# Attention scores in 4 MB tiles: turning keys and queries with 32x32 word blocks on VectorE instead of TensorE transposes

## The chip, the cores and the metric

The kernel runs on one core of a Trainium2 chip. The metric is the device time of one execution in microseconds (us), the median over several runs of the same program. One further execution is taken with the hardware profiler; its own time and span stand in the table below.

## What is computed

```
batch, heads, seq, dim = 8, 8, 512, 64
scale = 1.0 / np.sqrt(q.shape[-1])
return (np.einsum('bhqd,bhkd->bhqk', q, k) * scale).astype(np.float32)
```

For each of the 64 heads (8 batches of 8) a 512 x 512 matrix of scaled dot products is made from 512 queries and 512 keys of 64 elements. The inputs q and k are 8.39 MB each, the output is 67.11 MB, all float32 in DRAM.

## The kernel before

**Units, loads, words.** Two batches make a unit, and there are four (`UNITS`). A unit's keys and queries come in with one transfer of 2 MB each (`load`, L82; the very first is split in two halves, L87, one on SyncE's queue and one on ScalarE's). Each of the 128 partitions gets 64 consecutive rows of one head, 16 KB in one piece; partition p holds piece p of the unit in DRAM order (`k_r`, `q_r`). GpSimd casts them to bfloat16 (L131, 16 casts of 2048 elements a partition) and lays two rows side by side, so that one 32-bit word holds the same element of two rows (`xb`). A transpose that moves 32-bit words thus turns two rows at once. Each load's casts raise `ready` by one when they are done.

**Turning.** TensorE contracts over partitions, so keys and queries must lie with their 64 elements along partitions. `turn` (L139) transposes eight 128 x 128 blocks of words on TensorE, with an identity matrix that GpSimd makes at the start (L108 and L110), into a PSUM tile (`tp`; at the start also the score tiles). A unit has four such chunks, two of keys and two of queries. `move` (L191) copies each chunk from PSUM into `kT` (keys) and `qz` (queries): ScalarE copies one half and VectorE the other, two copies each. `qz` is zero outside its blocks (two memsets, L197), so that one matmul over 128 partitions makes 64 queries of two heads, whose keys lie in the upper and lower 64 partitions of `kT`.

**Scores and output.** The output is written in 16 tiles of 4 MB, four heads each (`out_r`). A tile has eight pairs of matmuls (`scores`, L154); each pair fills one of three PSUM tiles (`ps`, 128 x 1024 float32). ScalarE takes the even pairs (L218) and VectorE the odd ones (L221): they scale and write to one of three SBUF buffers of 4 MB (`big`). SyncE (SP) waits for both engines' four drains (L100 and L101) and stores the tile with one transfer (L102). The three `big` buffers also receive the loads of the units (`xf`), the second of them twice.

**What sets the order.** Everything is written out by hand, engine by engine, with semaphores. SP's queue holds the loads, then the wait for casts that free the buffer of the last unit's two loads, then the 16 stores in order. A tile's buffer is free when its casts are done (tiles 0 to 2) or the store three tiles earlier has landed; TensorE waits for that itself, between the two matmuls of the tile's first pair. In tile g, TensorE also turns chunk g + 4 after the third pair (while there is one), and both drain engines move it between their drains.

Of the kernel before, what the change touches and what calls it, by code (L numbers as in the profile page):

```python
# [5 lines left out]
def kernel(  # L6
# [5 lines left out]
    nc = tc.nc  # L12
    B, H, S, D = q.shape
    scale = 1.0 / (D ** 0.5)
    P = 128
    UNITS = B // 2
    N = H
    M = P // (2 * H)
    R = S // M
    J = R // 2  # L20
    RO = 8
    U = S // RO
    JP = J // 2
    JJ = J // RO // 2
    W = 8
    IW = W // JJ
    TILES = N // 2
    CHUNKS = 4
    SLOTS = 12
    PAIRS = RO  # L30

    f32 = mybir.dt.float32
    bf16 = mybir.dt.bfloat16
    mult = mybir.AluOpType.mult


    names = ["ready", "moved", "zeroed", "ident", "turn", "pe_act", "pe_dve", "act", "dve"]
    sem = {name: nc.alloc_semaphore(name) for name in names}
    load_sems = [nc.alloc_semaphore(f"load{n}") for n in range(2 * UNITS)]
    halves = [load_sems[0], nc.alloc_semaphore("load0b")]  # L40
    store_sems = [nc.alloc_semaphore(f"store{n}") for n in range(3)]
    ALL = CHUNKS * UNITS

    q_r = q.rearrange("(v b) g (m j) d -> v (b g m) (j d)", b=2, j=R)
    k_r = k.rearrange("(v b) g (m j) d -> v (b g m) (j d)", b=2, j=R)
    out_r = out.rearrange("(v b) (t x h) (u i) k -> (v b t) (h u) x (i k)", b=2, x=2, h=2, i=RO)

    bigs = [nc.alloc_sbuf_tensor(f"big{n}", [P, 2, RO, S], f32)[:] for n in range(3)]
    xb = nc.alloc_sbuf_tensor("xb", [P, SLOTS * W, 2, D, 2], bf16)[:]
    kT = nc.alloc_sbuf_tensor("kT", [P, 2 * N, M, 2, J], bf16)[:]  # L50
    qz = nc.alloc_sbuf_tensor("qz", [P, 2 * N, RO, P], bf16)[:]
    identity = nc.alloc_sbuf_tensor("identity", [P, P], f32)[:]
    tp = nc.alloc_psum_tensor("tp", [P, W, P], f32)[:]
    pss = [nc.alloc_psum_tensor(f"ps{n}", [P, 2, S], f32)[:] for n in range(3)]

    def words(ap):
        return ap.bitcast(f32)

    def half(h):
        return slice(h * D, (h + 1) * D)  # L60

    kw = words(kT)
    qw = words(qz)
    xw = words(xb.rearrange("p w s d e -> p w (s d e)"))
    keys = kT.rearrange("p n m s j -> p n (m s j)")

    pe = nc.tensor

# [4 lines left out]
    def store_buffer(g):  # L75
        return bigs[(0, 2, 1)[g % 3]]

    def rows(v, x):
        return (k_r, q_r)[x][v].rearrange("p (s c) -> p s c", s=2)

    def load(v, x):
        nc.sync.dma_start(out=xf(v)[:, x], in_=rows(v, x)).then_inc(load_sems[2 * v + x], 16)  # L82

    for s, queue in enumerate((nc.sync, nc.scalar)):
        first_load = queue.dma_start(out=xf(0)[:, 0, s], in_=rows(0, 0)[:, s]  # L87
                                     ).then_inc(halves[s], 16)
        tc.no_tile_sem_insts.add(first_load.ins.name)
    tc.close()  # L90
    tc.compile()  # L91


    for n in range(1, 2 * (UNITS - 1)):
        load(n // 2, n % 2)
    for x in range(2):
        nc.sync.wait_ge(sem["ready"], 3 + x)
        load(UNITS - 1, x)
    for g in range(ALL):
        nc.sync.wait_ge(sem["act"], 4 * g + 4)  # L100
        nc.sync.wait_ge(sem["dve"], 4 * g + 4)  # L101
        nc.sync.dma_start(out=out_r[g], in_=store_buffer(g).rearrange("p x i k -> p x (i k)")  # L102
                          ).then_inc(store_sems[g % 3], 16)
    for n in range(3):
        nc.sync.wait_ge(store_sems[n], 16 * len(range(n, ALL, 3)))


    nc.gpsimd.memset(identity, 0.0).then_inc(sem["ident"], 1)  # L108
    nc.gpsimd.wait_ge(sem["ident"], 1)
    nc.gpsimd.affine_select(out=identity, in_=identity, compare_op=mybir.AluOpType.not_equal,  # L110
                            fill=1.0, base=0, pattern=[[-1, P]], channel_multiplier=1
                            ).then_inc(sem["ident"], 1)
    for v in range(UNITS):
        for x in range(2):
            w0 = (v * CHUNKS + 2 * x) % SLOTS * W
            if v or x:
                nc.gpsimd.wait_ge(load_sems[2 * v + x], 16)
            if v == UNITS - 1 and x == 0:
                nc.gpsimd.wait_ge(sem["turn"], CHUNKS)
            for s in range(2):  # L120
                if v == x == 0:
                    nc.gpsimd.wait_ge(halves[s], 16)
                src = xf(v)[:, x, s]
                dst = xb[:, w0:w0 + JP, s]
                if x == 0:
                    src = src.rearrange("p (j e d) -> p j e d", e=2, d=D)
                    dst = dst.rearrange("p j d e -> p j e d")
                else:
                    src = src.rearrange("p (j e i d) -> p j e i d", e=2, i=RO, d=D)
                    dst = dst.rearrange("p (i j) d e -> p j e i d", i=RO)  # L130
                cast = nc.gpsimd.tensor_copy(out=dst, in_=src)  # L131
            cast.then_inc(sem["ready"], 1)


    first = [tp] + [ps.rearrange("p w (c k) -> p (w c) k", k=P) for ps in pss]

    def turn(c, dst):
        for w in range(W):
            ins = pe.transpose(out=dst[:, w], identity=identity, in_=xw[:, c % SLOTS * W + w])  # L139
        ins.then_inc(sem["turn"], 1)  # L140

    def scores(g, p):
        x, i = p // 4, p % 4 * 2
        n = g % (2 * TILES) * 2 + x
        pair = PAIRS * g + p
        if pair >= 3:
            pe.wait_ge(sem["act" if p % 2 else "dve"], (pair - 3) // 2 + 1)
        for w in range(2):
            if p == 0 and w == 1:
                if g < 3:  # L150
                    pe.wait_ge(sem["ready"], (2, 6, 8)[g])
                else:
                    pe.wait_ge(store_sems[g % 3], g // 3 * 16)
            ins = pe.matmul(out=pss[pair % 3][:, w, :], lhsT=qz[:, n, i + w], rhs=keys[:, n],  # L154
                            start=True, stop=True)
        ins.then_inc(sem["pe_dve" if p % 2 else "pe_act"], 1)

    pe.wait_ge(sem["ident"], 2)
    for c in range(CHUNKS):
        if c % 2 == 0:  # L160
            pe.wait_ge(sem["ready"], c // 2 + 1)
        turn(c, first[c])
    pe.wait_ge(sem["moved"], 2)
    for g in range(ALL):
        c = g + CHUNKS
        for p in range(3):
            scores(g, p)
        if c < ALL:
            pe.wait_ge(sem["ready"], c // 2 + 1)
            turn(c, tp)  # L170
        for p in range(3, PAIRS):
            scores(g, p)

    def move(copy, c, s, tile_):
        v, t = divmod(c, CHUNKS)
        n0 = v % 2 * N
        h0 = t % 2 * W
        if t < 2:  # L180
            src = tile_[half(s)].rearrange("d j (n h m) -> d h n m j", n=N, h=2)
        else:
            src = tile_[half(s)].rearrange("d (i jj) (n h m) -> d h i n m jj", jj=JJ, n=N, h=2)
            h0 = t % 2 * IW
        for h in range(2):
            if t < 2:
                dst = kw[half(h), n0:n0 + N, :, s, h0:h0 + W]
            else:
                dst = qw[half(h), n0:n0 + N, h0:h0 + IW, h * U // 2:(h + 1) * U // 2].rearrange(
                    "d n i (m s jj) -> d s i n m jj", s=2, jj=JJ)[:, s]  # L190
            last = copy(out=dst, in_=src[:, h])  # L191
        return last

    def evacuator(engine, copy, scaled, parity, done, freed):
        if parity:
            for v in range(2):
                engine.memset(qz[:, v * N:(v + 1) * N], 0.0).then_inc(sem["zeroed"], 1)  # L197
        for c in range(CHUNKS):
            engine.wait_ge(sem["turn"], c + 1)
            if c == 2:  # L200
                engine.wait_ge(sem["zeroed"], 2)
            last = move(copy, c, parity, first[c])
        last.then_inc(sem["moved"], 1)
        count = 0
        for g in range(ALL):
            o = store_buffer(g)
            for p in range(parity, PAIRS, 2):
                x, i = p // 4, p % 4 * 2
                count += 1
                engine.wait_ge(done, count)  # L210
                scaled(o[:, x, i:i + 2, :], pss[(PAIRS * g + p) % 3]).then_inc(freed, 1)
                c = g + CHUNKS
                if p in (1, 2) and c < ALL:
                    engine.wait_ge(sem["turn"], c + 1)
                    move(copy, c, parity, tp)

    evacuator(nc.scalar, nc.scalar.copy,
              lambda o, ps: nc.scalar.mul(out=o, in_=ps, mul=scale),  # L218
              0, sem["pe_act"], sem["act"])
    evacuator(nc.vector, nc.vector.tensor_copy,  # L220
              lambda o, ps: nc.vector.tensor_scalar(out=o, in0=ps, scalar1=scale, scalar2=None,  # L221
                                                    op0=mult),
              1, sem["pe_dve"], sem["dve"])


# [28 lines left out]
```

## Time and profile before

| quantity | value |
|---|---|
| median of 3 runs | 201.21 us (201.21 to 202.08) |
| profiled execution, whole time | 201.47 us |
| profiled execution, span | 200.1 us |
| busy TensorE, VectorE, ScalarE, GpSimd | 100.0, 106.1, 84.8, 39.5 us |
| matmuls for scores (L154) | 256 issued, 249 recorded, 456 ns each |
| mean granted TensorE clock | 0.81 of full speed |
| transfers | 83.95 MB, mean 420 GB/s over the span |
| SP's store issues (L102) | 16, of 4096 KB, 0.37 us each |

The span is what the profiler covers; the whole time holds some 1.4 us more. A line number such as L154 is the line of the kernel that issued the instruction. Busy time of an engine that nobody waits for costs nothing; the view called the chain of waits follows back, from the last instruction, what each step was released by.

### The profile page before, as it was taken

What the parts mean: (1) busy time and instruction counts of PE and PEld (TensorE: products, weight loads), DVE (VectorE), ACT (ScalarE), POOL (GpSimd) and SP (SyncE); (2) the same over time, 40 slices, a digit from 0 to 9 for tenths busy, and PEclk for the clock granted to TensorE, in tenths of its full rate; (3) what the DMA queues carried; (4) which work ended last, traced back from release to release, by engine and by line L of the source; (5) the groups of instructions that cost most, each with busy time, mean ns of one, the idle gap of its engine ahead of it and who ended that gap; (6) DMA issues with size and microseconds to landing.
All of it is one profiled execution on the core that took longest, in us unless ns stands there. A gap on an engine that the chain in (4) does not pass through costs nothing.

```text
span 200.1 us, 1063 instructions
## 1 busy us (share of the span) xinstructions
PE 100.0 (50%) x377; PEld 47.2 (24%) x384; DVE 106.1 (53%) x98; ACT 84.8 (42%) x97; POOL 39.5 (20%) x22
## 2 busy tenths in 40 slices
PE   0027760376674757654764486366747374830000
PEld 0026530143231414311431243042202120200000
DVE  4815592076993757691769276829454435450000
ACT  2004671265773746572666266546444344430000
POOL 1299999995000000000000000000000000000000
PEclk9999997579998888995799679969697858585555
DMA  6999999999999999999999999999999999999995
GB/s 188 434 432 439 432 426 426 426 406 442 426 422 426 449 431 421 426 442 432 422 422 439 436 429 422 439 436 429 422 426 449 429 422 422 439 436 426 429 429 252
DMA packets 5653, 83.95 MB, mean 420 GB/s; under 512 B 400, under 2 KB 400, under 8 KB 400
## 3 DMA queue, kind: packets, MB, share of 16 engines
q1 hardware_dynamic: 5504, 82.84, 97.4%
q10 hardware_dynamic: 144, 1.05, 1.3%
q8 instruction: 3, 0.05, 0.1%
q14 instruction: 2, 0.02, 0.0%
HBM read 16.78 MB, written 67.11 MB: 419 GB/s over the span
## 4 chain that ended last, share of the span: by engine, by line
DMA 56%; DVE 12%; PE 10%; POOL 10%; issue 1%; SPq 0%
DMA out_dram<-big 43%; POOL xb L131 10%; DVE big L221 9%; PE ps L154 8%; DMA big<-in_k_dram 7%; DMA big<-in_q_dram 6%; PE tp L139 2%; DVE qz L191 2%; DVE kT L191 1%; SPq L101 0%
## 5 line engine op out<-in xcount | busy, mean ns | idle before, releaser
L154 PE MATMUL ps<-kT,qz 128*128 128x512 bf16 x249 | 80.2, 456 | 61.8 <-DMA out_dram<-big 32.4
L221 DVE TENSOR_SCALAR big<-ps 128x1024 f32<-128x1024 f32 x64 | 76.9, 1222 | 52.9 <-PE ps L154 48.6
L218 ACT ACTIVATE big<-ps 128x1024 f32<-128x1024 f32 x64 | 65.0, 1023 | 71.8 <-PE ps L154 66.4
L154 PEld LDWEIGHTS ps<-kT,qz 128*128 128x128 bf16 x256 | 25.3, 110 | 109.8 <-DMA out_dram<-big 35.8
L131 POOL CAST xb<-big 128x2048 bf16<-128x2048 f32 x16 | 38.8, 2467 | 6.5 <-DMA big<-in_k_dram 6.2
L139 PE MATMUL tp<-identity,xb 128*128 128x128 f32 x104 | 18.8, 341 | 13.7 <-POOL xb L131 13.7
L139 PEld LDWEIGHTS tp<-identity,xb 128*128 128x128 f32 x104 | 17.2, 185 | 17.7 <-issue 16.6
L191 DVE COPY kT<-tp 64x512 f32<-64x512 f32 x14 | 9.7, 694 | 10.2 <-PE tp L139 9.9
L191 ACT COPY kT<-tp 64x512 f32<-64x512 f32 x14 | 8.1, 577 | 14.8 <-PE tp L139 14.7
L191 DVE COPY qz<-tp 64x512 f32<-64x512 f32 x12 | 8.3, 694 | 3.0 <-PE tp L139 2.7
L197 DVE MEMSET qz<- 128x4096 uint32 x2 | 6.9, 3472 | 3.6 <-PEq L91 2.8
L191 ACT COPY qz<-tp 64x512 f32<-64x512 f32 x12 | 7.5, 624 | 1.2 <-PE tp L139 1.1
L139 PE MATMUL ps<-identity,xb 128*128 128x128 f32 x24 | 5.6, 421 | 1.2 <-POOL xb L131 1.2
L139 PEld LDWEIGHTS ps<-identity,xb 128*128 128x128 f32 x24 | 5.0, 226 | 1.6 <-POOL xb L131 1.6
L191 DVE COPY qz<-ps 64x512 f32<-64x512 f32 x4 | 2.8, 695 | 2.1 <-PE ps L139 2.1
L191 ACT COPY qz<-ps 64x512 f32<-64x512 f32 x4 | 2.5, 625 | 2.5 <-PE ps L139 2.4
L191 ACT ACT_TABLE_LOAD x1 | 1.3, 1283 | 1.9 <-PEq L91 1.9
L191 DVE COPY kT<-ps 64x512 f32<-64x512 f32 x2 | 1.4, 694 | 0.3 <-PE ps L139 0.3
L191 ACT COPY kT<-ps 64x512 f32<-64x512 f32 x2 | 1.2, 578 | 0.6 <-PE ps L139 0.5
L108 POOL MEMSET identity<- 128x128 f32 x1 | 0.2, 204 | 1.5 <-POOLq L91 1.5
L110 POOL TENSOR_SCALAR_AFFINE_SELECT identity<-identity 128x128 f32<-128x128 f32 x1 | 0.3, 293 | 0.2 <-POOL identity L108 0.2
L238 POOL MEMSET const-float32-0.0<- 128x1 f32 x1 | 0.1, 98 | 0.2 <-issue 0.2
(3 smaller groups left out, 0.3 us busy)
## 6 DMA issues: line engine op xcount, KB each, us to landing
out_dram<-big SPq DMA_DIRECT2D x16, 4096.0 KB, 21.5
big<-in_q_dram SPq DMA_DIRECT2D x4, 2048.0 KB, 17.6
big<-in_k_dram SPq DMA_DIRECT2D x3, 2048.0 KB, 16.2
big<-in_k_dram ACTq DMA_DIRECT2D x1, 1024.0 KB, 8.2
big<-in_k_dram SPq DMA_DIRECT2D x1, 1024.0 KB, 8.0
```

What stands on the lines that cost most here:

```text
L108: nc.gpsimd.memset(identity, 0.0).then_inc(sem["ident"], 1)
L110: nc.gpsimd.affine_select(out=identity, in_=identity, compare_op=mybir.AluOpType.not_equal, fill=1.0, base=0, pattern=[[-1, P]], channel_m ...
L131: cast = nc.gpsimd.tensor_copy(out=dst, in_=src)
L139: ins = pe.transpose(out=dst[:, w], identity=identity, in_=xw[:, c % SLOTS * W + w])
L154: ins = pe.matmul(out=pss[pair % 3][:, w, :], lhsT=qz[:, n, i + w], rhs=keys[:, n], start=True, stop=True)
L191: last = copy(out=dst, in_=src[:, h])
L197: engine.memset(qz[:, v * N:(v + 1) * N], 0.0).then_inc(sem["zeroed"], 1)
L218: lambda o, ps: nc.scalar.mul(out=o, in_=ps, mul=scale),
L221: lambda o, ps: nc.vector.tensor_scalar(out=o, in0=ps, scalar1=scale, scalar2=None, op0=mult),
L238: nc = _bacc.Bacc("TRN2", target_bir_lowering=False, num_devices=1)
```

## The change

Loads and stores stay at the same sizes and counts, and so do casts, matmuls and drains. The order of rows in the loads, the path that turns keys and queries, and the control of the score loop are new:

- **Loads.** A partition still gets 64 consecutive rows (16 KB). But partition 64s + 32h + 4m + 2b + x now holds piece m of head 4x + 2s + h of batch b of the unit, so each quadrant of 32 partitions holds 8 pieces of 4 heads. The four partitions of a group (2b + x) read DRAM rows that are 512 KB apart, and the next group starts 16 KB further on. Output tiles hold heads two of which lie 4 heads apart (2 before).
- **Turning.** `turn`, `move`, the identity and `tp` are gone. VectorE transposes 32 x 32 blocks of words straight from `xb` to `kT` and `qz` in SBUF: per two tiles, two instructions for keys (64 partitions x 1024 words) and four for queries (32 partitions x 1024 words). The output is written with a step of 1 KB between neighbouring words for keys, 2 KB for queries. `kT` and `qz` are half as large; one memset remains. The transposes for the next two tiles are spread over VectorE's queue by `after`: in an even tile one after drain 1, one after drain 4, two after drain 6; in an odd tile two after drain 1.
- **Drains.** There are four PSUM score tiles. ScalarE takes five pairs of each tile, VectorE three (`takers`).
- **Loop.** TensorE runs a loop of four rounds over four tiles, with counters that are lowered again in the loop. SP, after issuing a tile's store, waits until the next tile's buffer is free and then raises `next0` or `next1`, for which TensorE waits at the tile's first matmul.

```diff
-    q_r = q.rearrange("(v b) g (m j) d -> v (b g m) (j d)", b=2, j=R)
-    k_r = k.rearrange("(v b) g (m j) d -> v (b g m) (j d)", b=2, j=R)
-    out_r = out.rearrange("(v b) (t x h) (u i) k -> (v b t) (h u) x (i k)", b=2, x=2, h=2, i=RO)
+    q_r = q.rearrange("(v b) (x s h) (m j) d -> v (s h m) (b x) (j d)", b=2, x=2, s=2, j=R)
+    k_r = k.rearrange("(v b) (x s h) (m j) d -> v (s h m) (b x) (j d)", b=2, x=2, s=2, j=R)
+    out_r = out.rearrange("(v b) (x s h) (u i) k -> v s b (h u) x (i k)", b=2, x=2, s=2, i=RO)
...
+    takers = ["act", "dve", "act", "act", "dve", "act", "dve", "act"]
...
+        nc.sync.wait_ge(sem["out"], 2 * (g + 1))
+        nc.sync.dma_start(out=out_r[g // 4, g // 2 % 2, g % 2],
+                          in_=store_buffer(g).rearrange("p x i k -> p x (i k)")
                           ).then_inc(store_sems[g % 3], 16)
+        if g < ALL - 1:
+            if g < 2:
+                nc.sync.wait_ge(sem["ready"], (6, 8)[g])
+            else:
+                nc.sync.wait_ge(store_sems[(g + 1) % 3], (g + 1) // 3 * 16)
+            nc.sync.sem_inc(sem[f"next{(g + 1) // 2 % 2}"], 1)
...
-    def turn(c, dst):
-        for w in range(W):
-            ins = pe.transpose(out=dst[:, w], identity=identity, in_=xw[:, c % SLOTS * W + w])
-        ins.then_inc(sem["turn"], 1)
...
+    with pe.Fori(0, ALL // 4):
+        for t in range(4):
+            two, r = divmod(t, 2)
+            for p in range(PAIRS):
+                n, i = t * 2 + p // 4, p % 4 * 2
+                if p == 0:
+                    pe.wait_ge(sem[f"next{two}"], r + 1)
+                elif p >= 4:
+                    name, count = frees[p - 4]
+                    pe.wait_ge(sem[f"{name}{two}"], r * (3 if name == "act" else 1) + count)
+                for w in range(2):
+                    ins = pe.matmul(out=pss[p % 4][:, w, :], lhsT=qz[:, n, i + w], rhs=kT[:, n],
+                                    start=True, stop=True)
...
+    def turn_keys(b, y):
+        s = b % 2 * 2 * Q
+        return nc.vector.transpose(
+            out=kw[2 * y * Q:2 * (y + 1) * Q, b % 2 * G:(b % 2 + 1) * G].rearrange(
+                "d g (m w) -> d w m g", w=J),
+            in_=xw[s:s + 2 * Q, b // 2 * 2, :, y * Q:(y + 1) * Q])
+
+    def turn_queries(b, y, h):
+        s = (b % 2 * 2 + h) * Q
+        d = (2 * y + h) * Q
+        return nc.vector.transpose(
+            out=qw[d:d + Q, b % 2 * G:(b % 2 + 1) * G, :, h * Q:(h + 1) * Q].rearrange(
+                "d g i (m jj) -> d i jj m g", jj=JJ),
+            in_=xw[s:s + Q, b // 2 * 2 + 1, :, y * Q:(y + 1) * Q].rearrange(
+                "p (i jj) d -> p i jj d", i=RO))
...
+    after = {(0, 1): 1, (0, 4): 1, (0, 6): 2, (1, 1): 2}
...
-        for h in range(2):
-            if t < 2:
-                dst = kw[half(h), n0:n0 + N, :, s, h0:h0 + W]
-            else:
-                dst = qw[half(h), n0:n0 + N, h0:h0 + IW, h * U // 2:(h + 1) * U // 2].rearrange(
-                    "d n i (m s jj) -> d s i n m jj", s=2, jj=JJ)[:, s]
-            last = copy(out=dst, in_=src[:, h])
-        return last
```

## The prediction

> **What bounds the kernel now.** I read the profile in this order: the slices of the span, the transfers, the chain of waits, then the groups of instructions. The slices come first because one row of them has no gap.
>
> ```profile
> PE   0027760376674757654764486366747374830000
> DVE  4815592076993757691769276829454435450000
> DMA  6999999999999999999999999999999999999995
> HBM read 16.78 MB, written 67.11 MB: 419 GB/s over the span
> ```
>
> Each digit is a 5 us slice in tenths. TensorE and VectorE come and go; the transfer engines are full from the second slice to the last but one. So I asked whether they run at one rate. The windows view (columns: window and length; busy time and count of PE, PEld, DVE, ACT, POOL; clock; DMA share; GB/s) says yes, in loads and in stores:
>
> ```profile
> 5.00:15.00 10.00, 1.25 (x6) 1.28 (x7) 4.79 (x2) 0.00 (x0) 6.12 (x3) 1.00 1.02 434
> 38.00:42.00 4.00, 3.86 (x14) 2.50 (x15) 1.23 (x1) 2.05 (x2) 3.92 (x3) 0.50 1.00 401
> 100.00:150.00 50.00, 29.92 (x114) 13.20 (x114) 31.52 (x30) 25.84 (x29) 0.00 (x0) 0.86 1.00 430
> ```
>
> 83.95 MB at 430 GB/s are 195.2 us; with some 2.8 us before the first byte (the first slice moves 188 x 5 = 940 KB, 2.2 us at 430) and 2.1 us after the last that is the span, 200.1 us. The chain of waits shows how far compute is from the limit:
>
> ```profile
> 61.78 21.31 DMA out_dram<-big
> 83.09 0.04 issue
> 83.14 1.25 PE ps L154 x5
> ...
> 86.72 3.59 DVE big L221 x3
> 90.31 0.02 issue
> 90.32 0.02 SPq L101
> 90.34 0.03 issue
> 90.37 21.91 DMA out_dram<-big
> ```
>
> A tile waits for its buffer's store to land (83.1), is computed in 7.2 us and issues its own store at 90.3, which lands after 21.9 us. A 4.19 MB store needs 9.75 us at 430 GB/s. What an issue costs beside the bytes follows from the first load: 2.1 MB issued at 0.74, first cast at 8.79, so 8.05 - 2.1/0.434 = 3.2 us. The other 21.9 - 9.75 - 3.2 = 9 us it stood in the queue: that is slack. Over all stores:
>
> ```profile
> DMA to landing us min/median/max: 16.5/21.5/23.0
> ```
>
> So the thinnest slack is 16.5 - 9.75 - 3.2 = 3.5 us. Compute costs nothing until it is that late, and a lasting loss needs more than 9.75 us a tile.
>
> **The change, part by part.** These rows give the prices (count, then busy us and mean ns of one):
>
> ```profile
> L221 DVE TENSOR_SCALAR big<-ps 128x1024 f32<-128x1024 f32 x64 | 76.9, 1222 | 52.9 <-PE ps L154 48.6
> L218 ACT ACTIVATE big<-ps 128x1024 f32<-128x1024 f32 x64 | 65.0, 1023 | 71.8 <-PE ps L154 66.4
> L131 POOL CAST xb<-big 128x2048 bf16<-128x2048 f32 x16 | 38.8, 2467 | 6.5 <-DMA big<-in_k_dram 6.2
> L139 PE MATMUL tp<-identity,xb 128*128 128x128 f32 x104 | 18.8, 341 | 13.7 <-POOL xb L131 13.7
> L191 DVE COPY kT<-tp 64x512 f32<-64x512 f32 x14 | 9.7, 694 | 10.2 <-PE tp L139 9.9
> L197 DVE MEMSET qz<- 128x4096 uint32 x2 | 6.9, 3472 | 3.6 <-PEq L91 2.8
> ```
>
> *Removed:* 128 TensorE transposes (18.8 + 5.6 us), 32 copies on each of VectorE (22 us) and ScalarE (19 us), one memset (3.5 us), the identity. All of it ends in the 9 us of slack, except at the start, costed below.
>
> *Added on VectorE:* 48 transposes of 1024 words a partition. No such row exists. Low end: the memset's rate, 3472/4 = 0.87 us. High end: a word is two bf16, and GpSimd's cast writes 2048 bf16 in 2.47 us. I take 1.22 us, the L221 row, which is nearest: same engine, 1024 words. The output pattern steps 1 KB between words; L191 read PSUM with a 512-byte step: from it to L221 are 528 ns for 512 words more, 1.03 ns a word, which leaves 694 - 528 = 0.17 us fixed in both, so that step cost nothing per word. VectorE's drains fall from 4 to 3 a tile: 3 x 1.22 + 3 x 1.22 = 7.3 us a tile, against 4 x 1.22 + 2 x 0.69 = 6.3 now. ScalarE has five drains, 5.1 us. TensorE's 16 matmuls stand 0.43 us apart at the half clock (loads of weights at 38.54, 38.97, 39.39 and 39.82 in the timeline; the window from 38 to 42 shows 0.50), 6.9 us, and one drain, so 8.1. All are under 9.75.
>
> *Start.* Query casts end at 18.6; VectorE has four query transposes left, 4.9 us, to 23.5 (first score now: 23.8). Tile 0: 1.2 us to its first bank, then three drains and two key transposes, 6.1 us, so its store goes out near 31 (now 31.25). Loads fill the queue to 2.8 + 16.78/0.430 = 42. Tiles 1 and 2 start when GpSimd's casts free their buffers (38.1, 48.0), as now, and take about 7.5 us: issued at 46 and 55.5, with the queue full to 51.7 and 61.5. Nothing runs dry. What is late next if it did: the buffer's own landing, so each later tile.
>
> *Moved:* SP, not TensorE, now waits for a buffer's store and then raises a semaphore; TensorE's first matmul of a tile, ScalarE and VectorE's first drain stand behind that. SP does it after its own store issue (0.37 us), so queued behind the wait is only the next store, which cannot be ready earlier. Say 0.2 us a tile; the 9 us cover it, without them it is 15 x 0.2 = 3 us. The wait for the last two loads keeps its place. The transposes wait for casts, with VectorE's drains queued behind them; these waits are met before they are reached (the casts end at 47.9, tile 2 starts at 48.0). GpSimd's wait for the first turns goes; no row of the waits shows that it held anything. The loop's branch falls between tiles, under the same cover.
>
> *Loads.* Same bytes, same 16 KB rows, but neighbouring partitions now read rows 512 KB apart, in a pattern with one more dimension. Issue: loads now take 0.33 to 0.53 us; the first stands at 0.39, so 0 to 0.14 us, all on the path; I take 0.1. Rate: no load of this kind is in the trace; the windows bound it by 434 (0.4 us less over 16.78 MB) and 401 GB/s (2.8 us more). I take no change, since the stores, in two pieces 2 MB apart, run at 430 as well as the loads.
>
> The Trainium skill speaks against this, in "DMA: Bandwidth & Descriptors", section "Latency and other measured facts": with rows 512 KiB apart from partition to partition it gives 207 GB/s in each direction where a padded layout has 214. This trace has no such load. By it the loads would take 3% longer, an estimate of 1.3 us from that page, and the sum would be 202.7.
>
> **Sum.** 200.1 + 0.1 - 0 = 200.2 span; with the 1.37 us around the profiled span (201.47 - 200.1) 201.57. The runs' median lies 0.26 under the profiled run, so 201.3; I say 201.4, for tiles that start a little late. Its own range is 200.3 to 202.2.
>
> **The rivals.**
> *Slower, loads.* The transfer engines read the new row order less well. For it: they have no spare time, so each 1% of load rate costs 0.39 us; 0.5% (1 us) is reached below 420 GB/s. Against: descriptors stay 16 KB. At 401 GB/s: 204.2. If rows crowd on half of the engines, 39 us more: 240.
> *Slower, transposes.* A pair of tiles has 6 drains and 6 transposes and 1.2 us until VectorE's first bank; two stores take 19.5 us, so it decides from (19.5 - 7.3 - 1.2)/6 = 1.83 us a transpose. At 2.47 us: 23.3 - 19.5 = 3.8 us, over seven pairs 27, less about 6 of slack: 222. For it: a step of 1 KB at each word written, which no VectorE row has. Against: L191's strided reads.
> *Faster, transfers.* If new addresses ran everything at the best window's 434: 83.95/434 is 1.8 us less, 199.6. Against: the stores' rows are as before but for pieces 4 MB apart instead of 2.
> *Not what it says.* If the copies had been on the end's path, removing them would gain; the chain passes them in the 7.2 us only, which wait in the queue anyway: 201.4.
>
> **How the numbers follow.** Forecast 0.48 (0.05 of it the last rival, which gives the same time); loads slower 0.25; transposes slower 0.14; transfers faster 0.13. A change under 0.5% (200.2 to 202.2) can't be told from none. So faster 0.13, same 0.48, slower 0.39. For the range I leave out transposes well above 1.83 us and crowded loads (0.16) and 0.04 below: 199.6 to 212. Likeliest: 201.4.
>
> **What will show it.** The DMA row stays 9s throughout; the first store goes out near 31 us; landing times keep a minimum above 13 us; transposes near 1.2 us; load windows at 430. Wrong if a digit under 9 stands inside the row (compute late), or if it is full at a lower GB/s in the first 42 us (loads).

## The result, and the profile after

The changed kernel takes 208.71 us (median of 4 runs, 208.47 to 209.88) against 201.34 us for the kernel before in the same comparison: 3.7% slower, ratio 1.037 with a 95% interval of 1.0323 to 1.0416. The profiled execution spans 207.5 us. That lies inside the range of the prediction, but not in its likeliest case: the rival "slower, transposes" came.

First, the slices of the span and the sums of the page, as they were read before:

```profile
DVE  3338969995999599959996899779996999265000
DMA  5999999999999999999997999799979998899998
HBM read 16.78 MB, written 67.11 MB: 404 GB/s over the span
DVE 68%; PE 9%; DMA 5%; POOL 3%; ACT 3%; SPq 2%; issue 1%; DVEq 0%
```

The transfer row, full to the end before, now falls to 7 or 8 from the 22nd slice on, about once for every pair of tiles, and VectorE's row is nearly full. A digit under 9 inside the transfer row is what the prediction named as the sign that compute comes late. The last line, the shares of the chain that ended last by engine, turned round: DMA had 56% and VectorE 12%, now VectorE has 68% and DMA 5%. The groups of instructions say why (count, then busy us and mean ns of one):

```profile
L199 DVE TENSOR_SCALAR big<-ps 128x1024 f32<-128x1024 f32 x48 | 57.8, 1219 | 22.5 <-PE ps L146 22.2
L165 DVE STREAM_TRANSPOSE qz<-xb 32x1024 f32<-32x1024 f32 x32 | 64.2, 2005 | 1.2 <-POOL xb L126 0.8
L157 DVE STREAM_TRANSPOSE kT<-xb 64x1024 f32<-64x1024 f32 x16 | 31.0, 1935 | 7.3 <-POOL xb L126 7.0
```

A transpose of 1024 words takes 1.94 us (keys) or 2.01 us (queries), where the prediction took 1.22. What this makes of a pair of tiles is seen in VectorE's timeline, from the first drain of one even tile to that of the next (start, length, instructions; in brackets the idle time before):

```profile
93.34 1.23 DVE L199 TENSOR_SCALAR big<-ps 128x1024 f32<-128x1024 f32 x1 [2.43 <-PE ps L146]
94.59 1.94 DVE L157 STREAM_TRANSPOSE kT<-xb 64x1024 f32<-64x1024 f32 x1
96.40 1.19 DVE L199 TENSOR_SCALAR big<-ps 128x1024 f32<-128x1024 f32 x1
97.61 1.89 DVE L157 STREAM_TRANSPOSE kT<-xb 64x1024 f32<-64x1024 f32 x1
99.51 1.22 DVE L199 TENSOR_SCALAR big<-ps 128x1024 f32<-128x1024 f32 x1
100.65 4.02 DVE L165 STREAM_TRANSPOSE qz<-xb 32x1024 f32<-32x1024 f32 x2
104.68 1.23 DVE L199 TENSOR_SCALAR big<-ps 128x1024 f32<-128x1024 f32 x1
105.94 4.01 DVE L165 STREAM_TRANSPOSE qz<-xb 32x1024 f32<-32x1024 f32 x2
109.96 2.36 DVE L199 TENSOR_SCALAR big<-ps 128x1024 f32<-128x1024 f32 x2
114.75 1.23 DVE L199 TENSOR_SCALAR big<-ps 128x1024 f32<-128x1024 f32 x1 [2.43 <-PE ps L146]
```

The pair takes 114.75 - 93.34 = 21.41 us, and the five pairs beside it between 21.38 and 21.42. It has one gap of 2.43 us, in which SP issues the finished store, TensorE starts the next tile and VectorE waits for its first PSUM tile. The chain of waits shows the steps of that gap, after the drains that end at 112.33:

```profile
112.34 0.37 SPq L97
...
112.83 1.90 PE ps L146 x4
114.73 0.02 issue
114.75 1.23 DVE big L199
```

Two stores take 19.5 us, so each pair is 1.9 us too long. That costs nothing as long as finished stores stand in the transfer queue; once the queue is used up, a store lands as fast as it can when it finds the engines free:

```profile
DMA to landing us min/median/max: 11.2/11.8/17.4
```

The minimum was 16.5 us and the median 21.5 before. Now the median lies 0.6 us above the minimum of 11.2 us: most stores find the queue next to empty.

### The profile page after: what moved, and what is told of

Same layout as the page of the kernel before. It is cut to its first block, busy times and chain, and to the rows that moved or that the text cites. A ratio compares the mean times of both kernels' runs of the same rounds, so it can differ in the third digit from the quotient of the medians.

```text
span 207.5 us, 799 instructions
## 1 busy us (share of the span) xinstructions
PE 89.5 (43%) x256; PEld 29.8 (14%) x256; DVE 154.8 (75%) x97; ACT 79.4 (38%) x81; POOL 38.8 (19%) x20
## 4 chain that ended last, share of the span: by engine, by line
DVE 68%; PE 9%; DMA 5%; POOL 3%; ACT 3%; SPq 2%; issue 1%; DVEq 0%
DVE qz L165 31%; DVE big L199 24%; DVE kT L157 13%; PE ps L146 9%; DMA big<-in_k_dram 5%; POOL xb L126 3%; ACT big L196 3%; SPq L97 1%; SPq L105 0%; DVEq L175 0%
## 5 line engine op out<-in xcount | busy, mean ns | idle before, releaser
L146 PE MATMUL ps<-kT,qz 128*128 128x512 bf16 x256 | 89.5, 519 | 99.4 <-SPq L105 66.8
L196 ACT ACTIVATE big<-ps 128x1024 f32<-128x1024 f32 x80 | 78.1, 1025 | 108.1 <-PE ps L146 108.0
L199 DVE TENSOR_SCALAR big<-ps 128x1024 f32<-128x1024 f32 x48 | 57.8, 1219 | 22.5 <-PE ps L146 22.2
L165 DVE STREAM_TRANSPOSE qz<-xb 32x1024 f32<-32x1024 f32 x32 | 64.2, 2005 | 1.2 <-POOL xb L126 0.8
L146 PEld LDWEIGHTS ps<-kT,qz 128*128 128x128 bf16 x256 | 29.8, 125 | 158.6 <-SPq L105 74.6
L157 DVE STREAM_TRANSPOSE kT<-xb 64x1024 f32<-64x1024 f32 x16 | 31.0, 1935 | 7.3 <-POOL xb L126 7.0
L180 DVE MEMSET qz<- 128x4096 uint32 x1 | 3.5, 3472 | 3.5 <-PEq L81 3.5
L222 POOL MEMSET const-float32-0.0<- 128x1 f32 x1 | 0.1, 99 | 0.2 <-issue 0.2
L222 POOL MEMSET const-bfloat16-1.0<- 128x1 bf16 x1 | 0.1, 102 | 0.0
L222 POOL MEMSET const-uint8-127<- 128x1 uint8 x1 | 0.1, 102 | 0.0
L222 POOL MEMSET const-float32-1.0<- 128x1 f32 x1 | 0.1, 98 | 0.0
## 6 DMA issues: line engine op xcount, KB each, us to landing
big<-in_k_dram ACTq DMA_DIRECT2D x1, 1024.0 KB, 10.6
```

The source lines that it names most:

```text
L146: ins = pe.matmul(out=pss[p % 4][:, w, :], lhsT=qz[:, n, i + w], rhs=kT[:, n], start=True, stop=True)
L157: return nc.vector.transpose(out=kw[2 * y * Q:2 * (y + 1) * Q, b % 2 * G:(b % 2 + 1) * G].rearrange("d g (m w) -> d w m g", w=J), in_=xw[s ...
L165: return nc.vector.transpose(out=qw[d:d + Q, b % 2 * G:(b % 2 + 1) * G, :, h * Q:(h + 1) * Q].rearrange("d g i (m jj) -> d i jj m g", jj=J ...
L180: nc.vector.memset(qz, 0.0).then_inc(sem["zeroed"], 1)
L196: freed = nc.scalar.mul(out=o, in_=ps, mul=scale)
L199: freed = nc.vector.tensor_scalar(out=o, in0=ps, scalar1=scale, scalar2=None, op0=mult)
```

## Experiments

The first theory was that VectorE sets the pace because the transposes are slow, and that they are slow because of the step with which they write (A). Its rivals: 32-bit words are slow to transpose whatever the pattern (B), or the loss lies elsewhere, in the loads' new row order or in the gate by SP (C).

**Where the 2 us come from.** A probe: the changed kernel with groups of VectorE instructions appended after its last drain (its whole time, 274 us, therefore says nothing).

```diff
+    for n in range(4):
+        dve.transpose(out=step(4), in_=source).then_inc(sem["probe"], 1)
+        count[0] += 1
+        dve.wait_ge(sem["probe"], count[0])
```

Here `step(n)` writes the 1024 words of one stretch of `kT` in an order in which neighbours in time lie n words apart.

> The changed kernel, with 16 groups of four VectorE instructions behind its last drain, each waiting for the one before: transposes of 1024 words on 64 partitions with output steps of 1, 2, 4, 8, 32 and 256 words, from spread and from dense input, on 32 and 128 partitions, of 512 words, of 1024 bf16 elements, and plain copies of 1024 words with steps 1, 2, 4, 32 and 256. Theory A (the 1 KB step between written words is what makes a transpose take 1.94 us): 1.1 to 1.25 us at step 1, rising to 1.9 at some step, and the copies rise with it. Theory B (a transpose of 32-bit words takes about 1.9 us for 1024 words whatever the pattern): 1.9 us at every step, about 1.0 us for 512 words, half for bf16, and the copies stay at 1.1 to 1.25 us or below.

Its groups; transposes with steps of 1 (L221), 2 (L229), 4 (L233), 8 (L237), 32 (L241) and 256 words (L245), then dense ones of bf16 (L261) and on 32 partitions (L249), and plain copies with steps of 2 (L269), 4 (L273) and 256 (L281):

```profile
L237 DVE STREAM_TRANSPOSE kT<-xb 64x1024 f32<-64x1024 f32 x4 | 8.0, 2010 | 0.1
L233 DVE STREAM_TRANSPOSE kT<-xb 64x1024 f32<-64x1024 f32 x4 | 7.9, 1983 | 0.1
L245 DVE STREAM_TRANSPOSE kT<-xb 64x1024 f32<-64x1024 f32 x4 | 7.7, 1920 | 0.1
L241 DVE STREAM_TRANSPOSE kT<-xb 64x1024 f32<-64x1024 f32 x4 | 7.6, 1894 | 0.1
...
L229 DVE STREAM_TRANSPOSE kT<-xb 64x1024 f32<-64x1024 f32 x4 | 4.9, 1237 | 0.1
L261 DVE STREAM_TRANSPOSE kT<-xb 64x1024 bf16<-64x1024 bf16 x4 | 4.9, 1236 | 0.1
L221 DVE STREAM_TRANSPOSE kT<-xb 64x1024 f32<-64x1024 f32 x4 | 4.9, 1236 | 0.1
...
L249 DVE STREAM_TRANSPOSE kT<-xb 32x1024 f32<-32x1024 f32 x4 | 4.9, 1232 | 0.1
L281 DVE COPY kT<-xb 64x1024 f32<-64x1024 f32 x4 | 4.7, 1174 | 0.1
L273 DVE COPY kT<-xb 64x1024 f32<-64x1024 f32 x4 | 4.3, 1068 | 0.1
...
L269 DVE COPY kT<-xb 64x1024 f32<-64x1024 f32 x4 | 2.7, 687 | 0.1
```

A holds, and not as a slope but as an edge: a step of 8 bytes costs nothing (1237 ns), one of 16 bytes costs 750 ns (1983), and longer steps hardly change that (1894 to 2010). A step of 12 bytes was not tried. B falls: dense words take 1236 ns, as long as bf16 elements. The width does not matter either; a 32-partition transpose takes as long as a 64-partition one, so the four query instructions move as much as two key instructions in twice the time. Nor do the other engines make the transposes slow: the probe's transposes with the keys' own step (L245, 1920 ns) ran from 227.68 us on, when no transfer and no other engine was busy, and in the kernel they take 1935.

The Trainium skill has a rule for such an edge, in "SBUF — State Buffer", section "Door 1: The DMA port swizzle (why `[64,N]` ≈ `[32,N]`)": neighbouring accesses run at full speed as long as they hit a 16-byte line of SBUF at least twice, and each that opens a new line pays. The probe agrees with two hits as the edge, between steps of 8 and 16 bytes, and gives the price. The same note puts the free stride at 4 fp32 words; if that is to include a step of 4 words, the measurement contradicts it (1983 ns).

**Only SBUF, and on which side?** The prediction had taken a read of PSUM with a 512-byte step as its sign. A second probe asks what such a step costs where.

> The changed kernel with eleven groups of four VectorE instructions behind its last drain, 64 partitions and 1024 words each. The prediction took a read of PSUM with a 512-byte step, which cost nothing, as a sign for writes to SBUF with a step. If steps cost the same on every side: copies that read SBUF with a step of 4 or 256 words slow from 0.69 to about 1.0 us as those that write so did, and a copy from PSUM read with a step of 4 or 128 words slows too. If only SBUF is touched: SBUF reads slow, PSUM reads stay at the dense copy's time (1.1 to 1.25 us). PSUM to SBUF with a written step of 4 and 128 words: if a written word of its own 16 bytes takes two cycles, 1.9 to 2.1 us as in the transposes; if the limit is of two words a cycle against one, 1.1 to 1.25 us. Transposes that write runs of 2 words with jumps: 1.24 us if two words in 16 bytes are enough, 1.9 if not; runs of 4: 1.24 us, as the keys of the kernel with heads innermost.

Copies from PSUM (ps) to SBUF: read with steps of 1 (L238), 4 (L242) and 128 words (L246), written with steps of 4 (L250) and 128 (L254). From SBUF (xb): read with steps of 1 (L222), 2 (L226), 4 (L230) and 256 words (L234). Transposes that write runs of 2 words and then jump (L258):

```profile
L250 DVE COPY kT<-ps 64x1024 f32<-64x1024 f32 x4 | 7.8, 1942 | 0.1
L254 DVE COPY kT<-ps 64x1024 f32<-64x1024 f32 x4 | 7.5, 1870 | 0.1
L258 DVE STREAM_TRANSPOSE kT<-xb 64x1024 f32<-64x1024 f32 x4 | 4.9, 1236 | 0.1
...
L238 DVE COPY kT<-ps 64x1024 f32<-64x1024 f32 x4 | 4.9, 1216 | 0.1
L242 DVE COPY kT<-ps 64x1024 f32<-64x1024 f32 x4 | 4.9, 1216 | 0.1
L246 DVE COPY kT<-ps 64x1024 f32<-64x1024 f32 x4 | 4.9, 1216 | 0.1
L234 DVE COPY kT<-xb 64x1024 f32<-64x1024 f32 x4 | 4.6, 1160 | 0.1
L230 DVE COPY kT<-xb 64x1024 f32<-64x1024 f32 x4 | 4.3, 1063 | 0.1
...
L222 DVE COPY kT<-xb 64x1024 f32<-64x1024 f32 x4 | 2.7, 685 | 0.1
L226 DVE COPY kT<-xb 64x1024 f32<-64x1024 f32 x4 | 2.7, 685 | 0.1
```

A step in the PSUM read of such a copy is free at the lengths tried, 4 and 128 words (1216 ns three times). A step of 16 bytes or more in SBUF makes an instruction take 1.5 to 1.7 times as long, on the read side (685 to 1063) and on the write side (1216 to 1942). Two neighbouring words per jump are enough to avoid it (1236). The price is not one fixed time per written word: a write with a step of 4 words adds 381 ns to a copy from SBUF (687 to 1068, the first probe) and 726 ns to one from PSUM. What makes it so stays open.

**Is that the whole loss?** Three kernels ran together. In the first, only the first batch group is turned; later tiles are scored from what lies in the buffers.

```diff
+    nc.vector.memset(kT, 0.0)
...
-            coming = steps(g // 2 + 1)
+            coming = iter(())
```

> VectorE turns only the first batch group; the transposes for all later tiles are left out (their scores are made from what lies in the two buffers, one half of them zero from a memset), all else as in the changed kernel: loads in the new row order, the gate by SP, the loop, the drains 5 to 3. If VectorE's transposes are the whole loss: 201 to 202 us, DMA row full, stores landing 20 us after issue. If the loads' new row order or the gate by SP costs something of the 7.4 us: 203 us or more, with a lower rate in the first 42 us or gaps.

The second writes the same words in the order of memory, so keys and queries lie in another order.

```diff
-                "d g (m w) -> d w m g", w=J),
+                "d g c -> d (g c)"),
...
-            out=qw[d:d + Q, b % 2 * G:(b % 2 + 1) * G, :, h * Q:(h + 1) * Q].rearrange(
-                "d g i (m jj) -> d i jj m g", jj=JJ),
+            out=qw[d:d + Q, b % 2 * G:(b % 2 + 1) * G, :, h * Q:(h + 1) * Q],
```

> All transposes write their words in the order of memory (keys: one run of 1024 words a partition; queries: runs of 32 words), so keys and queries lie in another order and the scores are those of permuted rows and mixed heads; the same number of instructions and words. Theory A (write step): transposes near 1.2 us and 201 to 202 us in total. Theory B (32-bit words): transposes stay near 1.95 us and the total near 208.7 us.

The third keeps the transposes and gives one of VectorE's drains to ScalarE.

```diff
-    takers = ["act", "dve", "act", "act", "dve", "act", "dve", "act"]
+    takers = ["act", "dve", "act", "act", "act", "act", "dve", "act"]
```

> Drain 4 of each tile goes to ScalarE, so that VectorE has two drains a tile instead of three; transposes as they are. If VectorE's time per pair of tiles sets the pace (6 x 1.22 + 6 x 1.98 + 2.2 idle = 21.4 us against 19.5 us for two stores), it falls to 4 x 1.22 + 6 x 1.98 + 2.2 = 19.0 us, below the stores, and the total to 201 to 202.5 us. If something else sets the pace (SP's gate, the loop), it stays above 206 us.

| kernel | median us | ratio to before (95%) | transposes, ns | store landing, median us |
|---|---|---|---|---|
| without later transposes | 201.12 | 0.9989 (0.9980 to 0.9999) | | 22.3 |
| dense writes | 201.24 | 1.0001 (0.9991 to 1.0011) | 1239, 1233 | 21.3 |
| drain 4 to ScalarE | 201.24 | 1.0003 (0.9993 to 1.0013) | 1948, 2007 | 16.8 |

The kernel before took 201.23 us beside them. Each of the three gives back all of the 7.4 us. C falls: loads in the new order, the gate by SP and the loop are in all three, so by themselves they cost nothing here. In the first, the windows (length; busy times; clock; DMA share; GB/s) show loads at the old rate, which was 434 in both windows:

```profile
5.00:15.00 10.00, 0.00 (x0) 0.00 (x0) 5.04 (x2) 0.00 (x0) 6.61 (x3) 1.00 1.02 436
15.00:25.00 10.00, 0.00 (x0) 0.00 (x0) 9.04 (x6) 0.00 (x0) 9.90 (x5) 1.00 1.01 431
```

The second and third reach the same time in different ways: one shortens a transpose, the other leaves it at 2 us and takes 2 x 1.22 us of drains from each pair (19.27 us a pair, 19.0 expected). So it is VectorE's sum per pair that counts, not the transposes as such. The first also shows the floor: with no transposes at all, the transfers alone take 201.1 us, and no version with these transfers can be expected to beat the kernel before by more than that 0.1%.

**Is the price per pair right?** Three more, each moving one term of the pair. One fills the gap: the first key transpose of an even tile is put ahead of the first drain.

```diff
-    after = {(0, 1): 1, (0, 4): 1, (0, 6): 2, (1, 1): 2}
+    after = {(0, 0): 1, (0, 4): 1, (0, 6): 2, (1, 1): 2}
...
             coming = steps(g // 2 + 1)
+            nc.vector.wait_ge(sem["pe"], pair)
```

> The first key transpose of each even tile moves ahead of VectorE's first drain (behind a wait for the matmuls of the tile before, which read the same buffer); same instructions and durations. In the changed kernel VectorE waits 2.43 us there once per pair of tiles for its first PSUM tile. If that wait is a term of the pace (12 + 7.3 + 2.4 = 21.4 us a pair, seen), it shrinks to about 0.5 us, the pair to 19.5 us, the length of two stores, and the total to 201 to 203 us. If the pace is set by the hand-over through SP, nothing changes: 207 to 209 us.

One stores keys with the four head pairs innermost, so that a transpose writes runs of 4 words and TensorE reads with a step.

```diff
-                "d g (m w) -> d w m g", w=J),
+                "d (m w g) -> d w m g", w=J, g=G),
...
+    keys = kT.rearrange("p a (c g e) -> p a g c e", g=G, e=2)
```

> Keys are stored with the four head pairs innermost, so that a transpose writes runs of 4 neighbouring words; TensorE then reads a head's keys as pairs of bf16 with a step of 16 bytes. Queries as in the changed kernel. If short runs keep the dense rate: key transposes 1.24 us, a pair of tiles 7.3 + 2 x 1.24 + 4 x 2.0 + 2.4 = 20.2 us, 0.7 us above two stores, total 201 to 204 us. If a run of 4 words is as slow as single words: 1.9 us and 208.7. If TensorE reads with the step at half rate, its 16 matmuls of a tile grow and its busy time per matmul doubles from 519 ns; the total would then be above 215 us.

And one gives VectorE a fourth drain per tile.

```diff
-    takers = ["act", "dve", "act", "act", "dve", "act", "dve", "act"]
+    takers = ["act", "dve", "act", "act", "dve", "dve", "dve", "act"]
```

> Drain 5 of each tile goes to VectorE (four drains each for VectorE and ScalarE), all else as in the changed kernel. If VectorE's time per pair sets the pace, the pair grows by 2 x 1.22 to 23.8 us and the total by 7 to 8 pairs x 2.44 = 17 to 19.5 us, to 226 to 228 us. If VectorE is not what sets it, less than half of that.

The pair is measured in each timeline between the first drains of even tiles; seven pairs count, since the last of the eight has nothing left to turn. The loss is against the kernel before in the same comparison (201.24 us; 201.34 for the changed kernel).

| kernel | pair, us | seven pairs over 19.5 | loss, us | difference |
|---|---|---|---|---|
| drain 4 to ScalarE | 127.09 - 107.82 = 19.27 | none | 0.0 | |
| gap filled | 112.38 - 91.83 = 20.55 | 7.4 | 203.61 - 201.24 = 2.4 | 5.0 |
| keys with heads innermost | 112.77 - 92.20 = 20.57 | 7.5 | 203.95 - 201.24 = 2.7 | 4.8 |
| changed kernel | 21.41 | 13.4 | 208.71 - 201.34 = 7.4 | 6.0 |
| fourth drain | 123.13 - 99.48 = 23.65 | 29.1 | 224.09 - 201.24 = 22.9 | 6.2 |

Ratios: 1.0135 (1.0074 to 1.0195), 1.0129 (1.0107 to 1.0151) and 1.1151 (1.1114 to 1.1188) for the three. The last column is read as the slack that the transfer queue gives before a long pair shows: 5 to 6 us, and nearly the same over a loss from 2 to 23 us. The landing times agree: the thinnest of the kernel before, 16.5 us, is 5.3 us above the 11.2 us of a store that finds the queue empty. One formula, seven times the excess of a pair less 5 to 6 us, holds for all of them.

The gap shrank as expected, but the other two numbers of that expectation were missed: the pair came down by 0.86 us to 20.55, not to 19.5, and the total to 203.61 us, not to between 201 and 203. The timeline shows where the rest went:

```profile
91.83 1.23 DVE L199 TENSOR_SCALAR big<-ps 128x1024 f32<-128x1024 f32 x1 [0.48 <-PE ps L146]
94.00 1.22 DVE L199 TENSOR_SCALAR big<-ps 128x1024 f32<-128x1024 f32 x1 [0.94 <-PE ps L146]
```

The gap shrank from 2.43 to 0.48 us, but a new one of 0.94 us opened before the second drain, whose PSUM tile TensorE had not filled yet; a transpose had covered that wait before.

The fourth drain's expectation was missed too: 23.65 us a pair instead of 23.8, and 224.09 us instead of 226 to 228. A drain straight after another adds 1.13 us, not 1.22 (three take 3.49 us together), and seven pairs that are longer by 2.24 us give 15.7 us, against 15.4 measured between this kernel and the changed one.

With the heads innermost the keys' transposes fell to 1240 ns, so a run of 4 words is as fast as a dense one. The pair came to 20.57 us instead of the expected 20.2, with a gap of 2.51 us and a second wait of 0.22 before the second drain. TensorE paid for it: its weight loads, one per matmul, stand 0.45 us apart even at full clock (the window from 84 to 86 us has clock 1.00):

```profile
84.14 0.12 PEld L147 LDWEIGHTS ps<-kT,qz 128*128 128x128 bf16 x1 [0.34 <-issue]
84.60 0.12 PEld L147 LDWEIGHTS ps<-kT,qz 128*128 128x128 bf16 x1 [0.34 <-issue]
85.05 0.12 PEld L147 LDWEIGHTS ps<-kT,qz 128*128 128x128 bf16 x1 [0.34 <-issue]
```

In the changed kernel four of them fit into 0.75 us at 52.36, some 0.2 us apart, also at clock 1.00:

```profile
52.36 0.75 PEld L146 LDWEIGHTS ps<-kT,qz 128*128 128x128 bf16 x4 [0.22 <-issue]
```

The expected 215 us did not follow, since 16 x 0.45 = 7.2 us a tile stay below the 9.75 us of a store.

## Why the prediction was right or wrong

The range held, but not by the sum that the prediction believed in: 201.4 us missed by 7.3 us. The range reached to 212 because it left room for slower loads and somewhat slower transposes, and that the result fell inside it is in part luck: two terms, the price of a transpose and the idle time of a pair, were both too small.

- **What bounds the kernel before: right.** Transfers, at 431 GB/s, also in every version whose pair is under 19.5 us. Compute cost nothing until it was late, and the whole removed work (transposes on TensorE, copies on two engines, a memset) brought nothing: 0.1 us at most, in the version without later transposes.
- **Price of a transpose: wrong, and this decided.** The step that failed is "from it to L221 are 528 ns for 512 words more ... so that step cost nothing per word". The arithmetic was right, but of a row that steps in its PSUM read and writes runs of eight neighbouring words to SBUF, so it held no sign of a stepped write; there a step of 16 bytes or more makes the instruction take 1.5 to 1.7 times as long. 1.22 us is right for a dense transpose (1.236); the changed kernel's write with 1 or 2 KB steps costs 1.94 and 2.01. The upper bound, 2.47 us, held. Dense writes give back all of the 7.4 us, the filled gap 5.1.
- **Rival "slower, transposes": right in its mechanism, its idle term too small.** It took 1.2 us until VectorE's first bank; 2.43 us were seen: 0.50 us until TensorE starts, because SP issues a store first, and 1.90 us for TensorE's first four matmuls, at a granted clock of 0.50 (window from 112.80 to 114.75). With that the point from which it decides is (19.5 - 7.3 - 2.4)/6 = 1.63 us, not 1.83. By the formula as it stood, 1.98 us a transpose give a pair of 20.4 us and no loss after the 6 us of slack; with 2.43 us it is 21.6 us and 7 x 2.1 - 6 = 9 us, against 7.4 measured. The 6 us of slack came out near the 5 to 6 measured, but the prediction gives no working for them. Its own thinnest slack was 3.5 us, with 3.2 us for an issue beside the bytes; a store that finds the queue empty lands after 11.2 us, which leaves 1.5 us beside its 9.75 and makes the thinnest slack 5.3.
- **The gate by SP: covered as said, but priced too low.** Priced at 0.2 us a tile; the way through SP takes 0.50 us (112.33 to 112.83), and once the cover was gone it became part of the 2.43 us of each pair. With that gap down to 0.48 us the pair was 20.55 us.
- **Loads: right in rate, wrong in issue.** The first issue takes 0.63 us (0 to 0.14 over 0.39 was the bound), yet the first data come no later: the first cast starts at 6.73 us, 8.79 before, and the casts of the first queries end at 18.6 us in both. The 3% that the prediction took from the Trainium skill, "DMA: Bandwidth & Descriptors", section "Latency and other measured facts", an estimate of 1.3 us, is not seen (the page's layout steps 512 KiB at every partition, this one only within groups of four): 201.12 us for the kernel with these loads and no late VectorE. The rival "slower, loads" is out by the same run.
- **Start: half right.** The first score came at 27.0 us instead of 23.5 and the first store at 36.5 instead of 31. The four slow query transposes (8.16 us instead of 4.9) explain the first; the store was held up further by the two slow key transposes of tile 0 and by a first bank after 1.9 us instead of 1.2. The slack there held, as said: the transfer row is full until the 21st slice.

## What to carry to other kernels

Price a moved layout step by the memory it steps in and by the side, read or write: the PSUM read here said nothing about the SBUF write, and a row that is nearest by engine and size can be far by access pattern. When a kernel is bound by transfers, compute has a budget per transfer; sum each engine against it, gaps at the tile's start included, and shift work to the engine that has room (here one drain) before touching the slow instruction. A stepped access can be moved to another engine, but that engine then pays it.

## What the runs showed that was not expected

- A 16-byte step in SBUF makes a VectorE instruction take 1.5 to 1.7 times as long, for reads and for writes, and longer steps hardly change that (transposes: 1894 to 2010 ns for 4 to 256 words, 1236 dense); a copy from PSUM that reads with 4 or 128 words' step is as fast as a dense one (1216 ns).
- TensorE's moving operand pays for such a step too: pairs of bf16 16 bytes apart take 0.45 us per matmul at full clock, some 0.2 us when dense.
- A copy from SBUF to SBUF moves 1024 words in 685 ns, a transpose or a copy from PSUM in 1.22 to 1.24 us.
- The first load's two halves, issued together on two queues, landed after 5.9 and 10.6 us in the changed kernel, and after 8.0 and 8.2 before. The total did not depend on it; why they part was not tried.
